# First mixer of a diffusion trunk: probabilities left unscaled, 1/sum applied to the output, two score pairs ahead

## The chip, the cores and the metric

One core of a Trainium2 chip runs the whole program. The metric is the device time of one execution in microseconds; the time before is the median of three runs. One further execution was profiled, and all rows below come from it.

## The reference, cut to what matters

A trunk of two layers works on 256 latent tokens of width 1024 with 256 context tokens beside them. Each layer is half a feed-forward block, a token mixer, and another half feed-forward block. The change lies in the mixer of the first layer only, which joins attention (8 query heads, 2 key and value heads of 64) with four groups of pooling channels:

```
q = rms_norm(q) ; k = rms_norm(k)            # per head of 64
q, k(latent) = rotated by row and column angles
sc = q . k * ATTN_SCALE                      # 256 queries, 512 keys (context + latent)
pr = softmax(sc) ; attn = pr @ v
pool: mean over 2, 4, 8, 16 neighbours minus the token itself, @ pool_w
x = x + gate * (concat(attn, pool) @ w_out)
```

Everything is fp32. Large products are done as three products of a high and a low part of each operand.

## The kernel before, in words

Activations lie transposed, channels on the 128 partitions and tokens on the free axis. A weight block of 128x2048 is loaded by SP's queue into one of two `raw` buffers (`load_w`, L125) and split in two halves: ScalarE casts the high part (L153), VectorE subtracts for the low part (L154). Three buffers each hold high and low parts. A product of 128 outputs over 1024 channels is 24 matmuls of 258 columns (`in_tiles`, `mm3`, L148 to L150). The 8 PSUM banks come from one pool (`bank`, L45).

The mixer (`mixer_a`, L298) projects keys and values first, then four blocks of 128 query channels (`q_proj`); a block t holds query head t (group 0, first 64 partitions) and head t + 4 (group 1, last 64). `k_norm` (L354) sums the squares of each head by a product with a block matrix, which leaves the sum on all 64 partitions, takes the root on ScalarE and the reciprocal on VectorE over 128x512 elements, and scales the keys. `q_rope` (L386) forms the queries' sums (L390) and rotates a block: two multiplications, one product with a permutation (L343), one addition, and a split. The keys' latent half is rotated in `k_rope`. `q_norm` gives the queries' factors, which enter later as the scale of the exponential.

The attention goes by rounds v = 0 to 7: block t = v // 2, query half b = v % 2. `score(v)` makes two score tiles of 128 queries x 512 keys, one per group, in a PSUM bank each (six products, L441); VectorE takes the row maximum (L445) and scales it (L446); ScalarE takes the exponential with the row sum as a second output (L448); VectorE takes the reciprocal of the sum (L450) and multiplies the 512 probabilities with it (L451). `turn(v)` transposes the eight 128x128 pieces on TensorE (L463), and ScalarE copies them to SBUF (L464). After both halves of a block, `attend(t)` multiplies with the values (L472), 64 outputs for each group, and splits the result from PSUM (L153, L154).

The loop issues `score(v + 1)` before `turn(v)`. Between these stand pieces of the pooling branch, listed in `fill`: `p_mm` (24 matmuls, L148 to L150), `p_proj` (VectorE and ScalarE) and `p_finish` (one product, L425). The weight blocks of the output projection are loaded and split in rounds 3, 5 and 6; their VectorE halves are pinned to the program's order. The fourth is loaded in `out_proj`, which follows with 8 x 24 matmuls.

The framework orders the instructions of each engine when the kernel is built: program order is the priority, and a planner with cost estimates lets an instruction go ahead when an earlier one isn't ready by its reckoning. Each engine then runs its list in order. Semaphores and buffer waits are set by the framework.

Of the kernel before, what the change touches and what calls it, by code (L numbers as in the profile page):

```python
# [9 lines left out]
F32 = mybir.dt.float32  # L10
F32R = mybir.dt.float32r
BF16 = mybir.dt.bfloat16
AF = mybir.ActivationFunctionType
ALU = mybir.AluOpType
AX = mybir.AxisListType

P = 128
D = 1024
NK = D // P
T = 256  # L20
# [11 lines left out]
K_BLK, K_ROT, K_COS, K_SIN, K_HSEL, K_END = 0, 128, 256, 512, 768, 770  # L32
# [3 lines left out]
def trunk(ctx: ExitStack, tc: tile.TileContext, I, out):  # L36
    nc = tc.nc
    V, S, PE = nc.vector, nc.scalar, nc.tensor
# [3 lines left out]
    tmp = ctx.enter_context(tc.tile_pool(name="tmp", bufs=1))  # L42
    pp = ctx.enter_context(tc.tile_pool(name="pp", bufs=8, space=bass.MemoryType.PSUM))

    def bank():  # L45
        return pp.tile([P, 512], F32, name="ps")
# [4 lines left out]
    ident = const.tile([P, P], F32, name="ident")  # L51
# [9 lines left out]
    epsb = const.tile([P, 1], F32, name="epsb")  # L61
# [90 lines left out]
    def split(hi, lo, src, pin=lambda ins: ins):  # L152
        S.copy(hi, src)  # L153
        pin(V.tensor_tensor(out=lo, in0=src, in1=hi.bitcast(F32), op=ALU.subtract))  # L154
# [143 lines left out]
    def mixer_a(after):  # L298
        with tc.tile_pool(name="mixa", bufs=1) as mp:
            poolw = mp.tile([P, 4, P], F32, name="poolw")  # L300
            cst = mp.tile([P, K_END], F32, name="cst")
            nc.sync.dma_start(out=cst, in_=I["cst"])
            blk = cst[:, K_BLK:K_BLK + P]
            rot = cst[:, K_ROT:K_ROT + P]
            cosT = cst[:, K_COS:K_COS + T]
            sinT = cst[:, K_SIN:K_SIN + T]
# [27 lines left out]
                                op=ALU.mult)  # L334
                return c

            def rotate(z):

                zs = tmp.tile([P, T], F32, name="hn", bufs=2)
                V.tensor_tensor(out=zs, in0=z, in1=sinT, op=ALU.mult)  # L340
                V.tensor_tensor(out=z, in0=z, in1=cosT, op=ALU.mult)
                ps = bank()
                PE.matmul(ps[:, :T], rot, zs, start=True, stop=True)  # L343
                V.tensor_tensor(out=z, in0=ps[:, :T], in1=z, op=ALU.add)
                return z

            def kv(mh, part, ps):
                z = (kz, vz)[mh][:, part]
# [3 lines left out]
                    S.activation(out=ksq[:, part], in_=z, func=AF.Square)  # L352

            def k_norm():  # L354
                ps = bank()
                PE.matmul(ps, blk, ksq, start=True, stop=True)
                S.activation(out=ksq, in_=ps.rearrange("p (a t) -> p a t", a=2), func=AF.Sqrt, scale=1.0 / 64, bias=epsb)
                V.reciprocal(ksq, ksq)
                V.scalar_tensor_tensor(out=kz, in0=kz, scalar=par[:, C_QK + 1:C_QK + 2],
                                       in1=ksq, op0=ALU.mult, op1=ALU.mult)  # L360

            def k_rope():
                rotate(kz[:, 0])
                split(KH, KL, kz)

            def v_turn():
                ps = bank()
                for i in range(4):
                    PE.transpose(ps[:, i * P:i * P + P],
                                 vz[:, i // 2, i % 2 * P:i % 2 * P + P], ident)  # L370
                S.copy(VV, ps.rearrange("p (i c) -> p i c", i=4))

            qz = {}

            def q_proj(t):
                z = mp.tile([P, T], F32, name="qz", bufs=4)
                sq = mp.tile([P, T], F32, name="qsq", bufs=4)
                c = proj(1 + t // 2, t % 2, z)
                S.activation(out=sq, in_=z, func=AF.Square, bias=c)
                g = par[:, C_QK:C_QK + 1]  # L380
                cg = mp.tile([P, 1], F32, name="col", bufs=8)
                V.tensor_tensor(out=cg, in0=c, in1=g, op=ALU.mult)
                S.activation(out=z, in_=z, func=AF.Identity, scale=g, bias=cg)
                qz[t] = (z, sq)

            def q_rope(t):  # L386
                z, sq = qz.pop(t)
                for b in range(2):
                    c = 4 * t + 2 * b
                    PE.matmul(qps[:, c:c + 2], sq[:, b * P:b * P + P], hsel, start=True, stop=True)  # L390
                split(QH[:, t], QL[:, t], rotate(z))

            def q_norm():
                q16 = qs.rearrange("p t b h -> p (t b h)")
                S.activation(out=q16, in_=qps[:, 0:16], func=AF.Sqrt, scale=1.0 / 64, bias=epsb)
                V.reciprocal(q16, q16)
                V.tensor_scalar(q16, q16, ATTN_SCALE, None, ALU.mult)
# [3 lines left out]
            def p_proj(gi):  # L401
                w = WINDOWS[gi]
                icnt = mp.tile([P, T], F32, name="icnt", bufs=2)
                nc.sync.dma_start(out=icnt, in_=I["icnt"][gi].partition_broadcast(P))
                pb = mp.tile([P, T + 16], F32, name="pb", bufs=2)
                nc.gpsimd.memset(pb[:, 0:8], 0.0)
                nc.gpsimd.memset(pb[:, 8 + T:], 0.0)
                mid = pb[:, 8:8 + T]
                c = proj(0, 0, mid, pps.pop(gi))
                S.activation(out=mid, in_=mid, func=AF.Identity, bias=c)  # L410
                cur, width, step = pb, T + 16, 1
                while step < w:
                    nxt = mp.tile([P, T + 16], F32, name="pw", bufs=2)
                    V.tensor_tensor(out=nxt[:, :width - step], in0=cur[:, :width - step],
                                    in1=cur[:, step:width], op=ALU.add)
                    cur, width, step = nxt, width - step, 2 * step
                st = 8 - w // 2
                pd = mp.tile([P, T], F32, name="pd", bufs=2)
                V.tensor_tensor(out=pd, in0=cur[:, st:st + T], in1=icnt, op=ALU.mult)
                V.tensor_tensor(out=pd, in0=pd, in1=mid, op=ALU.subtract)  # L420
                pds[gi] = pd
# [9 lines left out]

            pes, pts = {}, {}

            def score(v):
                t, b = v // 2, v % 2
                bs = slice(b * P, b * P + P)
                ps = [bank(), bank()]
                own = [slice(64 * g, 64 * g + 64) for g in range(2)]
                for i, (q, k) in enumerate(((QL, KH), (QH, KH), (QH, KL))):
                    for g in range(2):  # L440
                        PE.matmul(ps[g], q[own[g], t, bs], k[own[g]], start=i == 0, stop=i == 2)  # L441
                for g in range(2):
                    st = mp.tile([P, 3], F32, name="st", bufs=4)
                    sc = qs[:, t, b, g:g + 1]
                    V.reduce_max(out=st[:, 0:1], in_=ps[g], axis=AX.X)  # L445
                    V.tensor_scalar(st[:, 0:1], st[:, 0:1], sc, -1.0, ALU.mult, ALU.mult)  # L446
                    pe = tmp.tile([P, 2 * T], F32, name=("sa", "h32")[g], bufs=2)
                    S.activation(out=pe, in_=ps[g], func=AF.Exp, scale=sc, bias=st[:, 0:1],  # L448
                                 accum_out=st[:, 1:2])
                    V.reciprocal(st[:, 2:3], st[:, 1:2])  # L450
                    V.tensor_scalar(pe, pe, st[:, 2:3], None, ALU.mult)  # L451
                    pes[v, g] = pe

            def turn(v):
                t, b = v // 2, v % 2
# [10 lines left out]
            def attend(t):  # L466
                av = bank()
                pt = [pts.pop((t, g)) for g in range(2)]
                for i in range(4):
                    for g in range(2):  # L470
                        own = slice(64 * g, 64 * g + 64)
                        PE.matmul(av[own, :T], VV[:, i, own], pt[g][:, i], start=i == 0, stop=i == 3)  # L472
                split(OH[:, 4 + t], OL[:, 4 + t], av[:, :T])

            psk = in_tiles(*weights(0), (0, 1), (0, T + 2), T + 2, late=True)
            rstd()
# [6 lines left out]
            def p_mm(gi):  # L483
                pps[gi] = in_tiles(*weights(3 + gi // 2), (gi % 2,), (0,), T + 2)[0]

            k_norm()
            p_mm(0)
            qps = bank()
            q_rope(0)
            q_rope(1)  # L490
            p_mm(1)
            q_rope(2)
            v_turn()
            q_rope(3)
            k_rope()
            q_norm()
            score(0)
            p_proj(0)
            p_proj(1)
            fill = {0: lambda: p_mm(2), 1: lambda: (p_mm(3), p_finish(0), p_proj(2)),  # L500
                    2: lambda: (p_finish(1), p_proj(3)), 3: lambda: p_finish(2),
                    4: lambda: p_finish(3)}
            wout = []
            for v in range(8):
                if v in fill:
                    fill[v]()
                if v + 1 < 8:
                    score(v + 1)
                if v in (3, 5, 6):
                    wout.append(load_w(I["w_out_a"][len(wout)], 2048, tc.keep_in_program_order))  # L510
                turn(v)
                if v % 2 == 0 and v:
                    attend(v // 2 - 1)
# [290 lines left out]
```

## Time and profile before

| | |
|---|---|
| median of 3 runs | 1154.62 us (1152.18 to 1155.01) |
| profiled execution | 1152.68 us, span 1150.9 us |
| TensorE busy | 98% of the span |
| VectorE busy | 874.2 us, 76% |
| ScalarE busy | 521.6 us, 45% |
| mean granted TensorE clock | 0.999 |

The span runs from the first to the last instruction. Busy time counts an engine's instructions; ends of matmuls are modelled, so a matmul's pace is better read from start to start. The waits give idle time of an engine before an instruction and what released it. The first mixer's own work runs from about 407 us to about 503 us, its attention rounds from about 435 us to 480 us.

### The profile page before, as it was taken

The numbers are of one execution on the slowest core, as the hardware profiler recorded it, in microseconds if no ns is written. First come the engines' busy times: TensorE is split into PE (matmuls) and PEld (weight loads), VectorE is DVE, ScalarE is ACT, GpSimd is POOL, SyncE is SP. The second block draws the span as 40 slices with busy tenths as digits, with TensorE's granted clock in tenths as the row PEclk, the third lists the DMA queues.
The fourth block names the chain that finished last, engine by engine and source line by source line (L and its number), as shares of the span: only waits on it lengthen the run. The fifth ranks groups of instructions, "written<-read, shape, count | busy, mean of one in ns | idle before, by whom it ended". The sixth has DMA issues, their size and how long they took to land.

```text
span 1150.9 us, 19103 instructions
## 1 busy us (share of the span) xinstructions
PE 1132.6 (98%) x7646; PEld 1031.1 (90%) x7646; DVE 874.2 (76%) x1614; ACT 521.6 (45%) x814; POOL 68.4 (6%) x140
## 2 busy tenths in 40 slices
PE   8999999999999997899999999999999999999998
PEld 4878888888888895699999999999999899999998
DVE  5967787878789989778778788656767688756663
ACT  5552212222223456565334456434445866534442
POOL 0000110122222100000010000000000000000000
PEclk9999999999999999999999999999999999999999
DMA  8844656788888840556587656446546536546543
GB/s 318 309 147 156 194 185 232 275 299 317 303 289 303 318 159 10 183 183 219 180 312 261 229 193 219 162 155 225 184 142 247 185 132 210 182 152 226 179 146 116
DMA packets 52408, 242.72 MB, mean 211 GB/s; under 512 B 5600, under 2 KB 11488, under 8 KB 38880
## 3 DMA queue, kind: packets, MB, share of 16 engines
q1 hardware_dynamic: 33888, 174.39, 42.8%
q0 software_dynamic: 18432, 67.12, 17.5%
q8 instruction: 60, 0.98, 0.3%
q14 instruction: 28, 0.23, 0.1%
HBM read 240.44 MB, written 1.05 MB: 210 GB/s over the span
## 4 chain that ended last, share of the span: by engine, by line
PE 93%; DVE 4%; ACT 1%; DMA 1%; issue 1%; SPq 0%; ACTq 0%; DVEq 0%
PE ps L148 29%; PE ps L149 29%; PE ps L150 29%; PE ps L662 1%; PE ps L583 1%; PE ps L584 1%; PE ps L582 1%; PE ps L645 1%; DMA raw<-in_w 1%; PE ps L630 1%; DVE st L445 1%; DVE wlo L154 1%; DVE wm L80 1%; DVE junk L80 0%; PE ps L472 0%
## 5 line engine op out<-in xcount | busy, mean ns | idle before, releaser
L148 PE MATMUL ps<-AH,wlo 128*128 128x258 f32 (+2 forms) x1664 | 507.9, 306 | 0.3 <-ACT AH L153 0.3
L149 PE MATMUL ps<-AH,whi 128*128 128x258 f32 (+2 forms) x1664 | 507.2, 305 | 0.0
L150 PE MATMUL ps<-AL,whi 128*128 128x258 f32 (+2 forms) x1664 | 506.1, 305 | 0.0
L153 ACT CAST whi<-raw 128x1024 fp32r<-128x1024 f32 (+2 forms) x354 | 313.6, 921 | 364.5 <-PE ps L150 254.6
L154 DVE TENSOR_TENSOR wlo<-raw,whi 128x1024 fp32r<-128x1024 f32 (+2 forms) x354 | 367.7, 1065 | 53.6 <-ACT whi L153 52.8
L148 PEld LDWEIGHTS ps<-AH,wlo 128*128 128x128 f32 x1664 | 317.1, 191 | 16.3 <-issue 1.0
L149 PEld LDWEIGHTS ps<-AH,whi 128*128 128x128 f32 x1664 | 315.0, 189 | 14.7 <-issue 0.5
L150 PEld LDWEIGHTS ps<-AL,whi 128*128 128x128 f32 x1664 | 314.1, 189 | 14.2 <-DVE AL L154 0.2
L150 PE MATMUL ps<-HL,whi 128*128 128x256 f32 (+1 forms) x704 | 218.0, 310 | 0.0
L149 PE MATMUL ps<-HH,whi 128*128 128x256 f32 (+1 forms) x704 | 218.0, 310 | 0.0
L148 PE MATMUL ps<-HH,wlo 128*128 128x256 f32 (+1 forms) x704 | 218.0, 310 | 0.0
L80 DVE CUSTOM_DVE_ANT_0 wm<-wm,cc 128x1024 f32<-128x1024 f32 x138 | 165.0, 1221 | 6.1 <-DMA wm<-in_w_mod 5.4
L150 PEld LDWEIGHTS ps<-HL,whi 128*128 128x128 f32 x704 | 132.5, 188 | 7.8
L149 PEld LDWEIGHTS ps<-HH,whi 128*128 128x128 f32 x704 | 132.6, 188 | 7.7
L148 PEld LDWEIGHTS ps<-HH,wlo 128*128 128x128 f32 x704 | 132.5, 188 | 7.7
L72 POOL DMA_DIRECT2D wm<-in_w_mod x128 | 67.7, 529 | 553.8 <-DVE mod L80 507.0
L206 ACT ACTIVATE sa<-sa,cb 128x256 f32<-128x256 f32 x66 | 33.6, 510 | 120.4 <-DVE sa L205 117.0
L246 DVE SCALAR_TENSOR_TENSOR X<-ps,gate,X 128x256 f32<-128x256 f32 x64 | 30.9, 483 | 47.4 <-PE ps L150 47.2
L204 DVE COPY cb<-ps 128x1 f32<-128x1 f32 x66 | 10.3, 156 | 73.6 <-PE ps L150 73.5
L80 DVE CUSTOM_DVE_ANT_0 junk<-wm,cc 128x1024 bf16<-128x1024 f32 x34 | 41.5, 1219 | 8.8 <-ACT cc L632 8.1
L212 DVE TENSOR_TENSOR h<-ps,sa 128x512 f32<-128x512 f32 x22 | 15.2, 693 | 42.1 <-PE ps L150 33.6
L154 DVE TENSOR_TENSOR HL<-h,HH 128x256 fp32r<-128x256 f32 (+1 forms) x88 | 42.4, 485 | 0.0
(160 smaller groups left out, 709.5 us busy)
## 6 DMA issues: line engine op xcount, KB each, us to landing
raw<-in_w SPq DMA_DIRECT2D x84, 1024.0 KB, 4.9
wm<-in_w_mod POOLq DMA_DIRECT2D x128, 512.0 KB, 5.0
raw<-in_w SPq DMA_DIRECT2D x64, 704.0 KB, 4.1
wm<-in_w_mod SPq DMA_DIRECT2D x10, 512.0 KB, 6.9
raw<-in_w_in_a SPq DMA_DIRECT2D x5, 1024.0 KB, 8.5
raw<-in_w SPq DMA_DIRECT2D x8, 512.0 KB, 6.2
raw<-in_w_out_a SPq DMA_DIRECT2D x4, 1024.0 KB, 4.8
raw<-in_w_in_cu SPq DMA_DIRECT2D x4, 1024.0 KB, 4.9
```

What stands on the lines that cost most here:

```text
L72: eng.dma_start(out=w, in_=I["w_mod"][layer, i])
L80: pin(V.tensor_tensor_reduce(out=res, in0=w, in1=cc[:, st, :], scale=1.0, scalar=0.0, op0=ALU.mult, op1=ALU.add, accum_out=mod[:, 2 * laye ...
L148: PE.matmul(ps, wl, xh, start=first, stop=False)
L149: PE.matmul(ps, wh, xh, start=False, stop=False)
L150: PE.matmul(ps, wh, xl, start=False, stop=last)
L153: S.copy(hi, src)
L154: pin(V.tensor_tensor(out=lo, in0=src, in1=hi.bitcast(F32), op=ALU.subtract))
L206: S.activation(out=sa[:, :T], in_=sa[:, :T], func=AF.Silu, bias=cb[:, 0:1])
L212: V.tensor_tensor(out=h32[:, :n], in0=ps[1][:, :n], in1=sa[:, :n], op=ALU.mult)
L246: V.scalar_tensor_tensor(out=X[:, m, :T], in0=ps[:, :T], scalar=gate[:, 2 * layer, sub, m:m + 1], in1=X[:, m, :T], op0=ALU.mult, op1=ALU.add)
L445: V.reduce_max(out=st[:, 0:1], in_=ps[g], axis=AX.X)
L582: PE.matmul(ps[b], AL[:, k, ts], hi[:, ws], start=(k == 0), stop=False)
```

## The change

Probabilities stay unscaled: the row sums go to a tile `su` that lasts for the whole mixer, one reciprocal per block gives `ri`, and after the product with the values 1/sum is spread over partitions and applied to the output. The spread is a product: the column of 1/sum, broadcast to 64 columns, is the stationary operand and the identity the moving one, so that each of 64 output partitions gets the 128 values as a row. Four such products serve one block (two query halves, two groups). The keys' 1/rms is now computed on 128x8 elements (tokens on partitions) and spread in the same way by eight products. Rotations take two query blocks at a time. Scores are issued two rounds ahead of the transposes, the queries' sums come first, `p_mm(1)` and `p_mm(2)` stand elsewhere, and the output projection's weights are loaded in rounds 4 and 6, two blocks instead of three.

```diff
             def k_norm():
                 ps = bank()
-                PE.matmul(ps, blk, ksq, start=True, stop=True)
-                S.activation(out=ksq, in_=ps.rearrange("p (a t) -> p a t", a=2), func=AF.Sqrt, scale=1.0 / 64, bias=epsb)
-                V.reciprocal(ksq, ksq)
+                for i in range(4):
+                    PE.matmul(ps[:, 2 * i:2 * i + 2], ksq[:, i // 2, i % 2 * P:i % 2 * P + P], hsel,
+                              start=True, stop=True)
+                rk = mp.tile([P, 8], F32, name="rk")
+                S.activation(out=rk, in_=ps[:, 0:8], func=AF.Sqrt, scale=1.0 / 64, bias=epsb)
+                V.reciprocal(rk, rk)
+                return rk
+
+            def k_scale(rk):
+                ps = spread([rk[:, 2 * i:2 * i + 2] for i in range(4)])
                 V.scalar_tensor_tensor(out=kz, in0=kz, scalar=par[:, C_QK + 1:C_QK + 2],
-                                       in1=ksq, op0=ALU.mult, op1=ALU.mult)
+                                       in1=ps.rearrange("p (a t) -> p a t", a=2),
+                                       op0=ALU.mult, op1=ALU.mult)
+
+            def spread(cols):
+                ps = bank()
+                for i, c in enumerate(cols):
+                    for g in range(2):
+                        PE.matmul(ps[64 * g:64 * g + 64, i * P:i * P + P],
+                                  c[:, g:g + 1].broadcast_to([P, 64]), ident, start=True, stop=True)
+                return ps
...
+            def q_rope(h):
+                z = qz.pop(h)
+                rotate(z, 2)
+                split(QH[:, 2 * h:2 * h + 2], QL[:, 2 * h:2 * h + 2], z)
...
-                    pe = tmp.tile([P, 2 * T], F32, name=("sa", "h32")[g], bufs=2)
+                    pe = tmp.tile([P, 2 * T], F32, name="sa", bufs=2) if v % 3 == 2 else \
+                        mp.tile([P, 2 * T], F32, name="pe", bufs=4)
                     S.activation(out=pe, in_=ps[g], func=AF.Exp, scale=sc, bias=st[:, 0:1],
-                                 accum_out=st[:, 1:2])
-                    V.reciprocal(st[:, 2:3], st[:, 1:2])
-                    V.tensor_scalar(pe, pe, st[:, 2:3], None, ALU.mult)
+                                 accum_out=su[:, t, b, g:g + 1])
                     pes[v, g] = pe
+                if b == 1:
+                    V.reciprocal(ri[:, t], su[:, t])
...
-                split(OH[:, 4 + t], OL[:, 4 + t], av[:, :T])
+                ps = spread([ri[:, t, b] for b in range(2)])
+                rs = tmp.tile([P, T], F32, name="hn", bufs=2)
+                S.copy(rs, ps[:, :T])
+                V.tensor_tensor(out=rs, in0=av[:, :T], in1=rs, op=ALU.mult)
+                split(OH[:, 4 + t], OL[:, 4 + t], rs)
...
-            k_norm()
+            rk = k_norm()
             p_mm(0)
             qps = bank()
+            for t in range(4):
+                q_sums(t)
+            k_scale(rk)
             q_rope(0)
+            q_norm()
+            p_mm(1)
+            k_rope()
+            v_turn()
             q_rope(1)
-            p_mm(1)
-            q_rope(2)
-            v_turn()
-            q_rope(3)
-            k_rope()
-            q_norm()
             score(0)
+            p_mm(2)
+            score(1)
             p_proj(0)
             p_proj(1)
-            fill = {0: lambda: p_mm(2), 1: lambda: (p_mm(3), p_finish(0), p_proj(2)),
-                    2: lambda: (p_finish(1), p_proj(3)), 3: lambda: p_finish(2),
-                    4: lambda: p_finish(3)}
+            fill = {0: lambda: (p_mm(3), p_finish(0)), 1: lambda: (p_finish(1), p_proj(2)),
+                    2: lambda: p_proj(3), 3: lambda: p_finish(2), 5: lambda: p_finish(3)}
             wout = []
             for v in range(8):
+                if v + 2 < 8:
+                    score(v + 2)
                 if v in fill:
                     fill[v]()
-                if v + 1 < 8:
-                    score(v + 1)
-                if v in (3, 5, 6):
+                if v in (4, 6):
                     wout.append(load_w(I["w_out_a"][len(wout)], 2048, tc.keep_in_program_order))
                 turn(v)
```

`rotate` takes n blocks and reads its angle tables broadcast over them; `q_sums(t)` is the sums' part of the old `q_rope`.

## Rows read from the trace of the kernel before

**Rows 1.** The page's first part: busy us, share of the span, instructions.

```profile
PE 1132.6 (98%) x7646; PEld 1031.1 (90%) x7646; DVE 874.2 (76%) x1614; ACT 521.6 (45%) x814; POOL 68.4 (6%) x140
```

**Rows 2.** Stretches: from:to, length, busy by engine (instructions), granted clock, DMA share, GB/s.

```profile
421.40:441.68 20.28, 17.99 (x116) 15.21 (x115) 17.10 (x44) 13.39 (x25) 0.14 (x2) 0.92 0.18 59
441.68:479.28 37.60, 28.49 (x200) 18.46 (x200) 33.75 (x89) 25.19 (x55) 2.24 (x6) 1.00 0.33 118
```

**Rows 3.** TensorE's waits, 400 to 520: us in total, times, longest.

```profile
PE ps L463 <- DVE sa L451: 6.5, 5, 1.9
...
PE ps L463 <- DVE h L451: 1.5, 3, 1.1
```

**Rows 4.** Timeline of TensorE, 432 to 441: start, us, instruction [idle before <-releaser].

```profile
432.71 0.70 PE L343 MATMUL ps<-hn,cst 128*128 128x256 f32 x2 [0.71 <-DVE hn L340]
434.96 1.26 PE L441 MATMUL ps<-wm 64*128 64x512 f32 x6 [1.56 <-ACT wm L153]
436.16 0.58 PE L148 MATMUL ps<-AH,wlo 128*128 128x258 f32 x1
...
439.54 0.29 PE L148 MATMUL ps<-AH,wlo 128*128 128x258 f32 x1
...
440.51 0.29 PE L150 MATMUL ps<-AL,whi 128*128 128x258 f32 x1
```

**Rows 5.** Stretches of 1 us around the first scores, columns as in rows 2.

```profile
437.00:438.00 1.00, 1.00 (x6) 1.00 (x6) 1.00 (x5) 0.98 (x2) 0.00 (x0) 0.50 0.00 0
```

**Rows 6.** VectorE's groups, 421.4 to 482.05: instruction xcount | busy us, mean ns | idle before.

```profile
L154 DVE TENSOR_TENSOR wlo<-raw,whi 128x1024 fp32r<-128x1024 f32 x7 | 8.3, 1220 | 0.0
L451 DVE TENSOR_SCALAR h<-h,st 128x512 f32<-128x512 f32 x8 | 3.9, 484 | 0.1
L451 DVE TENSOR_SCALAR sa<-sa,st 128x512 f32<-128x512 f32 x8 | 3.9, 483 | 0.1
L358 DVE RECIPROCAL X<-X 128x512 f32<-128x512 f32 x1 | 3.4, 3353 | 0.9 <-ACT X L357 0.9
...
L450 DVE RECIPROCAL st<-st 128x1 f32<-128x1 f32 x16 | 2.6, 161 | 1.8 <-ACT sa L448 0.9 <-ACT h L448 0.3
...
L333 DVE TENSOR_TENSOR pb<-ps,rb 128x256 f32<-128x256 f32 x4 | 1.7, 416 | 0.0
```

**Rows 7.** ScalarE's groups, 421.4 to 482.05, columns as in rows 6.

```profile
L464 ACT COPY pt<-ps 128x512 f32<-128x512 f32 x16 | 9.0, 588 | 3.0 <-PE ps L463 3.0
...
L153 ACT CAST AH<-ps 128x256 fp32r<-128x256 f32 x4 | 1.5, 372 | 3.6 <-PE ps L472 3.6
```

**Rows 8.** Line L555 of the second mixer: ns min/median/max, first and last start.

```profile
L555 PE MATMUL ps<-wsp,VT x32: 273/275/377, 929.2 to 932.8; 128*128 128x128 f32 x32
```

**Rows 9.** Timeline of TensorE at 430 and 454, columns as in rows 4.

```profile
429.64 0.95 PE L390 MATMUL ps<-cst,qsq 128*128 128x2 f32 x8
430.45 0.68 PE L343 MATMUL ps<-hn,cst 128*128 128x256 f32 x2
430.97 0.60 PE L369 MATMUL ps<-ident,X 128*128 128x128 f32 x4
...
453.24 0.63 PE L463 MATMUL ps<-ident,h 128*128 128x128 f32 x4 [0.23 <-DVE h L451]
453.80 1.95 PE L472 MATMUL ps<-pt,VV 128*64 128x256 f32 x16
455.68 0.70 PE L425 MATMUL ps<-pd,poolw 128*128 128x256 f32 x2
```

**Rows 10.** Chain that ended last, 421 to 425: start, us, what.

```profile
421.40 0.86 PE ps L356 x2
```

**Rows 11.** Timelines of VectorE and ScalarE for one score pair, columns as in rows 4.

```profile
449.02 1.28 DVE L445 TENSOR_REDUCE st<-ps 128x1 f32<-128x512 f32 x2
...
451.94 0.20 ACT L448 ACTIVATION_READ_ACCUMULATOR h<-ps,st,qs 128x1 f32 x1
```

**Rows 12.** The page's DMA issues: queue, count, KB each, median us to landing.

```profile
raw<-in_w_out_a SPq DMA_DIRECT2D x4, 1024.0 KB, 4.8
```

More of the change, by code (lines that the diff above doesn't have):

```diff
@@ L302, in mixer_a @@
             nc.sync.dma_start(out=cst, in_=I["cst"])
-            blk = cst[:, K_BLK:K_BLK + P]
             rot = cst[:, K_ROT:K_ROT + P]
@@ L335, in proj, with rotate @@
                 return c
[L337 to L345, printed above, removed]
+            def rotate(z, n):
+                zs = tmp.tile([P, 2 * T], F32, name="h32", bufs=2)[:, :n * T]
+                zs3 = zs.rearrange("p (a t) -> p a t", a=n)
+                V.tensor_tensor(out=zs3, in0=z, in1=sinT.unsqueeze(1).broadcast_to([P, n, T]),
+                                op=ALU.mult)
+                V.tensor_tensor(out=z, in0=z, in1=cosT.unsqueeze(1).broadcast_to([P, n, T]),
+                                op=ALU.mult)
+                ps = bank()[:, :n * T]
+                PE.matmul(ps, rot, zs, start=True, stop=True)
+                V.tensor_tensor(out=z, in0=ps.rearrange("p (a t) -> p a t", a=n), in1=z, op=ALU.add)
             def kv(mh, part, ps):
@@ L355, in k_norm @@
                 ps = bank()
-                PE.matmul(ps, blk, ksq, start=True, stop=True)
-                S.activation(out=ksq, in_=ps.rearrange("p (a t) -> p a t", a=2), func=AF.Sqrt, scale=1.0 / 64, bias=epsb)
-                V.reciprocal(ksq, ksq)
-                V.scalar_tensor_tensor(out=kz, in0=kz, scalar=par[:, C_QK + 1:C_QK + 2],
-                                       in1=ksq, op0=ALU.mult, op1=ALU.mult)
+                for i in range(4):
[7 more added lines that the diff above has]
+                ps = spread([rk[:, 2 * i:2 * i + 2] for i in range(4)])
+                V.scalar_tensor_tensor(out=kz, in0=kz, scalar=par[:, C_QK + 1:C_QK + 2],
+                                       in1=ps.rearrange("p (a t) -> p a t", a=2),
[7 more added lines that the diff above has]
+                return ps
             def k_rope():
-                rotate(kz[:, 0])
+                rotate(kz[:, 0:1], 1)
                 split(KH, KL, kz)
@@ L371, in v_turn @@
                 S.copy(VV, ps.rearrange("p (i c) -> p i c", i=4))
-            qz = {}
+            qz, qsq = {}, {}
             def q_proj(t):
-                z = mp.tile([P, T], F32, name="qz", bufs=4)
+                if t % 2 == 0:
+                    qz[t // 2] = mp.tile([P, 2, T], F32, name="qz", bufs=2)
+                z = qz[t // 2][:, t % 2]
                 sq = mp.tile([P, T], F32, name="qsq", bufs=4)
@@ L383, in q_proj, with q_sums @@
                 S.activation(out=z, in_=z, func=AF.Identity, scale=g, bias=cg)
-                qz[t] = (z, sq)
-            def q_rope(t):
-                z, sq = qz.pop(t)
+                qsq[t] = sq
+            def q_sums(t):
+                sq = qsq.pop(t)
                 for b in range(2):
@@ L390, in q_rope @@
                     PE.matmul(qps[:, c:c + 2], sq[:, b * P:b * P + P], hsel, start=True, stop=True)
-                split(QH[:, t], QL[:, t], rotate(z))
+            def q_rope(h):
+                z = qz.pop(h)
+                rotate(z, 2)
+                split(QH[:, 2 * h:2 * h + 2], QL[:, 2 * h:2 * h + 2], z)
             def q_norm():
@@ L432, in mixer_a @@
             pes, pts = {}, {}
+            su = mp.tile([P, 4, 2, 2], F32, name="su")
+            ri = mp.tile([P, 4, 2, 2], F32, name="ri")
             def score(v):
@@ L442, in score @@
                 for g in range(2):
-                    st = mp.tile([P, 3], F32, name="st", bufs=4)
+                    st = mp.tile([P, 1], F32, name="st", bufs=6)
                     sc = qs[:, t, b, g:g + 1]
```

## The prediction

> **What bounds the kernel now.** I read the page's first part, then the busy time of each engine by stretches, then TensorE's waits, then the timelines of the mixer. TensorE is busy for 1132.6 us, 98% of the span [rows 1]: outside the first mixer there is next to nothing to gain. The stretches show where it stands: 20.28 less 17.99 = 2.3 us of idle time from the keys' sums (421.4) to the start of the attention rounds (441.7), and 37.60 less 28.49 = 9.1 us in the rounds, up to the last output product (479.3) [rows 2]. That is 11.4 us. The waits say for whom: 8.0 us are transposes (L463) that wait for VectorE's scaling of the probabilities (L451) [rows 3]. In the rounds VectorE is busy 33.75 of 37.60 us [rows 2]: they are VectorE's, and TensorE takes its pace.
>
> A further loss is no idle time. The timeline shows TensorE waiting 0.71 and 1.56 us around the keys' rotation, with little work between, and then 15 products of 258 columns from 436.16 to 439.54, 0.225 us each, where the next eight, to 440.51, take 0.12 each [rows 4]. The granted clock there is 0.50, the lower of its two levels, 1.2 GHz [rows 5]; in the rounds it is 1.00 [rows 2]. Fifteen products at 0.12 are 1.8 us; 3.4 went by: 1.6 lost.
>
> **The change part by part.**
>
> *Normalising moved onto the output.* Gone are 16 multiplications of 128x512 (L451, 3.9 + 3.9 us) and 16 reciprocals (L450, 2.6). Added on VectorE are 4 reciprocals (at L450's 0.16: 0.6) and 4 multiplications by 1/sum out of PSUM (at L333's 0.42: 1.7) [rows 6]: 8 us less. With one weight block fewer in the rounds (two L154 halves, 2.4) about 23 of 33.75 are left, and VectorE no longer sets the pace. ScalarE gets 4 copies of 128x256 out of PSUM (0.37 as L153's [rows 7]: 1.5) on its 25.19.
>
> *The price on TensorE*: four identity products with 64 outputs and 128 columns per head block and eight for the keys, 24 in all, each fp32 and so two records. No row shows this form. From above: L555 has the same 128 columns, but 128 outputs; its 32 records go from 929.2 to 932.8, 0.116 each, 0.23 a product, 5.6 for 24 [rows 8]. From below: L472 has the same half-array form on 256 columns; its 16 records fill 453.80 to 455.68, 0.117 each, where a full-array fp32 record of 256 columns (L343) takes 0.26 (two from 430.45 to 430.97) [rows 9]: two halves run at once. Half the columns at that pace are 0.06, 0.12 a product, 2.9 in all. I take 0.15 (nearer to L472, whose form it is): 1.2 for the keys and 2.4 for the output, 3.6.
>
> A change of form costs nothing that the trace shows: the L472 group begins 0.56 after four transposes that are 0.63 long by their own record (453.24) [rows 9]. The Trainium skill (TensorEngine Tiling (Array Packing), Key Properties) says that a change of tiling mode drains TensorE, which speaks against 64-output products between full ones. By it the keys' spread would pay two such drains and the output's none, as they follow L472 in its own mode; the trace puts no gap there, and the sum keeps its terms.
>
> *Keys' 1/rms on 8 columns.* Gone: the reciprocal of 128x512 (3.35 us of VectorE, L358 [rows 6]), which stands before the rotations of the queries in its queue, and L356's two records (0.86 us). Added: four products of two columns; eight records of that kind (L390) filled 429.64 to 430.45, 0.81, so the trade on TensorE is nought [rows 9, 10]. The root and the reciprocal shrink to 8 columns. The scaling itself stays and now waits for the spread, behind p_mm(0) and the queries' sums; behind it in VectorE's queue stands the first rotation, and for that waits TensorE's rotation product. The cover: VectorE has lost 3.35 us of work before that point, and TensorE has p_mm(1)'s 2.9 us to go on with. I cost it at nothing; without the cover it would be the keys' scaling and two multiplications, 1.6 us at some 0.7, 0.42 and 0.42.
>
> *Rotation by pairs.* The queries' twelve VectorE instructions of 256 columns become six of 512, and four splits become two: fewer fixed parts, the same elements, all beside TensorE's work. Nothing is counted, up or down by 0.5 us.
>
> *Order.* p_mm(1), 24 products of 0.12, moves to behind the first rotation, so that the keys' rotation runs beside 2.9 us of products; p_mm(2) stands between the first two score pairs. I count the 2.3 us of idle time and the 1.6 of lower clock as gone, less 0.3 for the keys' split, which the first scores still wait for.
>
> *Two score pairs ahead.* From the start of a pair's two reduces (449.02) to the end of its second exponential's sum (451.94 + 0.20) it is 3.1 us [rows 11]. Between a pair's scores and its transposes then stand another pair's scores (about 1), two transposed blocks (1.1 by 453.24), half an output with its spread (1.2) and mostly a fill: 3.3 us or more, and the normalising that followed is gone. So the rounds lose most of their 9.1 us. What stays: the last block's copy before the last output products; the tail (copy, multiply, cast, subtract at 0.37, 0.42, 0.37, 0.42: 1.6 us against 2.5 us of output projection that needs no result of it); and rounds in which two halves of a weight block (2.4) stand before a reduce in VectorE's queue. I leave 1.7 us for all, somewhat under the longest of today's waits (1.9 [rows 3]).
>
> *Weights of the output projection.* Three blocks are split in the rounds now, two then. SP's queue carries these loads and then those of the next stage through two raw buffers, so the third and fourth block and the next stage's first start when a split ends. A load lands 4.8 us after its issue [rows 12], its split takes some 3.6 more (three halves at L154's 1.2, since casts run beside subtractions); the third block is wanted 11.5 us into the projection (96 products of 0.12). That leaves 3 us even if its load began with the projection. Cost nothing; without the cover each us late is one lost.
>
> **Sum** against the profiled execution (1152.68 us, 1.8 of it outside the span): 11.4 + 1.6 - 3.6 - 0.3 - 1.7 = 7.4 us less, 1145.3. The median of the runs is 1.9 above that execution; against it the forecast is 1147.2.
>
> **The rivals.**
>
> *ScalarE takes over the rounds.* It is busy 25.19 of 37.60 us and gains 1.5. Its waits for transposes (L464, 3.0 us) and for output products (L153, 3.6) [rows 7] are a round trip with TensorE that a second pair ahead doesn't shorten. If 6.6 of TensorE's 9.1 us stay on that account, the gain is 2.5 - 2.4 in the rounds and 2.3 + 1.6 - 1.2 - 0.3 in front, 2.5 us: 1152.1. For it: weight casts stand in ScalarE's queue too. Against: today's waits name VectorE.
>
> *Slower: PSUM banks.* The pool has eight. Two score pairs hold four, p_mm(2) and p_mm(3) two until rounds 1 and 2, a transposed pair two, an output with its spread two. In rounds 0, 1, 2, 4 and 6 that is all of them, and the next product waits until a pair's exponentials are through, 3.1 us [rows 11]. Five such waits are 15.5; 15.5 + 3.6 - 11.4 - 1.6 = 6.1 us slower, 1160.7. It decides from 9.4 us of such waits on. Against it: with VectorE's 8 us gone, a pair's exponentials end before the pair two further on is due. The Trainium skill (PSUM — Partial Sum Buffer, Summary: rules for kernel authors) asks to evacuate promptly; here the sums of p_mm(2) and p_mm(3) lie through a round and more.
>
> *It doesn't do what it says.* The order on each engine is a planner's; today it joined the sums of two query blocks (eight L390 records in a row at 429.64 [rows 9]), between which the code has a rotation. It may place p_mm(1) and p_mm(2) so that the low clock stays (1.6) with 2.3 us of idle time: gain 3.5, 1151.1.
>
> *Better than forecast*: products at 2.9 and nothing left over, 11.4 + 1.6 - 2.9 = 10.1: 1144.5. The modelled ends of products before a wait (four transposes that are 0.63 long but step by 0.56) may hide a little more idle time at each: 2 us over the rounds at most, 1142.5.
>
> **How the numbers follow.** Forecast 0.5 (its own range 1144.5 to 1150), better 0.17, ScalarE 0.14, planner 0.09, banks 0.1. What can be told from no change is 0.3%, 3.5 us: under 1151.1 is faster. Forecast and better hold 0.67; half of the planner's case and a fourth of ScalarE's come to it: 0.75. The rest of these two is the same, with a bank case of few waits: 0.16. Slower 0.09. The range goes from the better case, 1142, to just under the median, 1154.
>
> **What would show it.** Right: no L451, no stretch at 0.50 around the first scores, TensorE's waits from 421 to the end of the rounds under 3 us and none for VectorE over 1, score pairs two ahead of their transposes, spread products at 0.12 to 0.23 us. Wrong: waits of score products or of p_mm's first product for exponentials (banks), of transposes for them (ScalarE), or output-projection products that wait for the third weight block.

## The result, and the profile after

The changed kernel takes 1141.76 us (median of 4, 1141.21 to 1142.81) against 1153.55 of the kernel before (median of 4): a ratio of 0.9899, 95% interval 0.9881 to 0.9916. That is some 11.7 us less (11.8 by the medians), where 7.4 was forecast, and 0.24 us below the range. The profiled execution took 1142.17 us, 10.5 less than that of before.

The page's first part and the stretches (columns as in [rows 1, 2]; from the keys' sums to the second scores, then to the end of the last output product):

```profile
PE 1132.2 (99%) x7696; PEld 1033.9 (91%) x7696; DVE 863.6 (76%) x1582; ACT 522.0 (46%) x816; POOL 68.4 (6%) x140
```

```profile
420.37:437.49 17.12, 16.71 (x130) 14.23 (x128) 13.13 (x34) 11.98 (x21) 0.14 (x2) 1.00 0.20 70
437.49:468.41 30.92, 30.04 (x236) 22.41 (x235) 26.98 (x67) 26.09 (x60) 2.23 (x6) 1.00 0.31 117
```

VectorE's load in the rounds fell from 33.75 us [rows 2] to 26.98; the two cuts do not hold quite the same work, as the new one takes in the second scores. From the keys' sums to the first result of the output projection, the same work but for the change, VectorE is busy for 41.15 us, before for 51.44. TensorE is busy for 30.04 of 30.92. Its waits in the mixer are down from 11.3 us to 1.3 in three pieces, none of them for VectorE (columns as in [rows 3]; L501 is the output product, L469 the scores):

```profile
PE ps L501 <- ACT pt L493: 0.9, 2, 0.5
PE ps L469 <- ACT wm L153: 0.4, 1, 0.4
```

TensorE's timeline (columns as in [rows 4]) has the new products, L377, for the keys and for one output, and products of 258 columns right behind the first scores:

```profile
425.93 1.09 PE L377 MATMUL ps<-ident,rk 128*64 128x128 f32 x16
426.95 1.12 PE L345 MATMUL ps<-h,cst 128*128 128x512 f32 x2
...
433.12 0.73 PE L469 MATMUL ps<-wm 64*128 64x512 f32 x4 [0.41 <-ACT wm L153]
...
434.98 0.28 PE L149 MATMUL ps<-AH,whi 128*128 128x258 f32 x1
435.10 0.29 PE L150 MATMUL ps<-AL,whi 128*128 128x258 f32 x1
...
455.44 1.95 PE L501 MATMUL ps<-pt,VV 128*64 128x256 f32 x16
457.21 0.61 PE L377 MATMUL ps<-ident,ri 128*64 128x128 f32 x8
457.75 0.96 PE L469 MATMUL ps<-wm 64*128 64x512 f32 x6
...
461.02 0.65 PE L501 MATMUL ps<-pt,VV 128*64 128x256 f32 x2
461.50 0.38 PE L377 MATMUL ps<-ident,ri 128*64 128x128 f32 x2
...
464.01 1.09 PE L492 MATMUL ps<-ident,pe 128*128 128x128 f32 x8
```

The keys' 16 records fill 425.93 to 426.95, 0.064 each, and an output's 8 fill 457.21 to 457.75. That output with its spread takes 2.31 us (455.44 to 457.75). The next one comes in pieces and takes 2.99 (461.02 to 464.01), though the view of waits lists nothing there. The 258-column products start every 0.12 us, at a granted clock of 1.00, where those of [rows 4, 5] ran at 0.50:

```profile
435.00:436.00 1.00, 1.00 (x11) 1.00 (x10) 1.00 (x3) 1.00 (x1) 0.00 (x0) 1.00 0.09 16
```

To compare executions I take one stretch in each trace: from the first record of the keys' sums to the first result of the output projection (L292). It is split into TensorE's waits as the view gives them, the time lost at the low clock (length times 1 less the granted clock, by half microseconds), and the rest, which is work and whatever idle time the view doesn't list, as under modelled ends. Before: 421.24 to 482.1. After: 420.37 to 471.6.

| kernel | stretch | waits (count) | lost at 0.50 | rest |
|---|---|---|---|---|
| before, profile at hand | 60.9 | 11.3 (11) | 1.7 | 47.9 |
| before, repeated | 62.4 | 11.3 (11) | 3.4 | 47.7 |
| before, once more | 62.2 | 11.3 (11) | 3.4 | 47.5 |
| after | 51.2 | 1.3 (3) | 0 | 49.9 |
| front_only | 59.6 | 9.1 (10) | 1.7 | 48.8 |
| rounds_only | 53.4 | 3.2 (4) | 1.7 | 48.5 |
| one_ahead | 57.4 | 5.0 (7) | 1.7 | 50.7 |
| scaled | 54.9 | 5.1 (5) | 1.7 | 48.1 |
| spread_twice | 54.2 | 1.6 (3) | 0 | 52.6 |
| seven_banks | 51.0 | 1.1 (3) | 0 | 49.9 |
| attend_late | 50.7 | 1.9 (3) | 0 | 48.8 |
| pmm_moved | 63.3 | 12.3 (12) | 3.4 | 47.6 |
| keys_wide | 52.4 | 2.1 (3) | 1.7 | 48.6 |
| keys_wide_late | 52.1 | 3.5 (5) | 0.3 | 48.3 |

Stretches are read in one execution each; ratios below are timed against the kernel before on the same chip. Executions of the same code before the mixer differ too: the stretch began between 419.86 and 421.63 in these fourteen traces. From its end to the end of the span it is 668.8 to 669.2 us in thirteen of them, so that a span is the start of the stretch, its length and a constant; in `keys_wide_late` it is 670.1, as most of its low stretch lies behind the end of the stretch.

### The profile page after: what moved, and what is told of

It reads as the page before. It is cut to its first block, busy times and chain, and to the rows that moved or that the text cites. A ratio compares the mean times of both kernels' runs of the same rounds, so it can differ in the third digit from the quotient of the medians.

```text
span 1140.4 us, 19165 instructions
## 1 busy us (share of the span) xinstructions
PE 1132.2 (99%) x7696; PEld 1033.9 (91%) x7696; DVE 863.6 (76%) x1582; ACT 522.0 (46%) x816; POOL 68.4 (6%) x140
## 4 chain that ended last, share of the span: by engine, by line
PE 97%; DVE 1%; ACT 1%; DMA 1%; issue 0%; SPq 0%; DVEq 0%; ACTq 0%
PE ps L148 30%; PE ps L149 30%; PE ps L150 30%; PE ps L697 1%; PE ps L618 1%; PE ps L619 1%; PE ps L617 1%; PE ps L680 1%; PE ps L665 1%; DMA raw<-in_w_out_a 0%; ACT whi L153 0%; PE ps L501 0%; PE ps L469 0%; DVE st L473 0%; PE ps L172 0%; ACT pe L477 0%
## 5 line engine op out<-in xcount | busy, mean ns | idle before, releaser
L154 DVE TENSOR_TENSOR wlo<-raw,whi 128x1024 fp32r<-128x1024 f32 (+2 forms) x354 | 367.6, 1064 | 54.4 <-ACT whi L153 53.4
L246 DVE SCALAR_TENSOR_TENSOR X<-ps,gate,X 128x256 f32<-128x256 f32 x64 | 30.9, 482 | 48.0 <-PE ps L150 47.9
```

Of the source, the lines that this page charges most:

```text
L246: V.scalar_tensor_tensor(out=X[:, m, :T], in0=ps[:, :T], scalar=gate[:, 2 * layer, sub, m:m + 1], in1=X[:, m, :T], op0=ALU.mult, op1=ALU.add)
```

## The experiments

**The two halves.** `front_only` is the changed front with the old rounds, `rounds_only` the reverse.

```diff
 front_only, against the changed kernel
-    (score, turn, attend and the loop of the changed kernel)
+    (those of the kernel before)
 rounds_only, against the kernel before
-    (score, turn, attend and the loop of the kernel before)
+    (those of the changed kernel, and spread)
```

> The keys' and queries' front of the changed kernel with the rounds of the kernel before (scaled probabilities, one pair ahead, weight blocks in rounds 3, 5 and 6). Theory (TensorE's idle time and its low clock in front are a gain of their own): first scores 1.0 us sooner after the keys' sums, no stretch at 0.50, the products of p_mm(2) at 0.12 again, 1.6 to 1.9: 2.5 to 3.5 us faster than before. Rival (front and rounds don't add, since VectorE's rounds take what the front gives): under 1 us faster. Rival (the low clock stays, as it comes with the rounds): 1 us faster and a row at 0.50.

> The front of the kernel before with the rounds of the changed one (unscaled probabilities, spread on the output, two pairs ahead, weight blocks in rounds 4 and 6). Theory: the rest of the 9.6 us by which the stretch from the keys' sums to the first output projection result got shorter, 6 to 7.5 us faster than before, with 0.7 and 1.6 us of waits at the keys' rotation and a stretch at 0.50 as before. Rival (parts don't add): either under 5 or over 8.5.

Measured: `front_only` 1150.65 us, 0.9973 (0.9962 to 0.9985), some 3.1 less; `rounds_only` 1145.13, 0.9923 (0.9911 to 0.9936), some 8.9 less. They add to 12.0 against 11.7 for both, so the halves are additive in time, within the intervals. The rounds' 8.9 lies above the 6 to 7.5 expected, while its stretch, 7.4 shorter than that of the profile at hand, lies within; against the two repeats below it is 9.0 and 8.8 shorter. In the traces they don't do what I expected one by one. The front alone shortened its stretch by 1.3 against the profile at hand, not 2.5 to 3.5 (against the repeats by 2.8 and 2.6): its waits fell by 2.2 and the low clock left the first scores, but it came back in the rounds, behind a wait of 1.9, in this execution (columns as in [rows 2]):

```profile
458.00:459.00 1.00, 1.00 (x6) 0.99 (x6) 1.00 (x2) 0.93 (x3) 0.00 (x0) 0.50 0.00 0
459.00:460.00 1.00, 1.00 (x6) 0.65 (x6) 1.00 (x2) 0.73 (x2) 0.00 (x0) 0.50 0.08 16
460.00:461.00 1.00, 1.00 (x6) 0.48 (x4) 1.00 (x4) 0.37 (x1) 0.00 (x0) 0.50 0.00 0
```

The rounds of [rows 2] had a clock of 1.00 with the same products and waits. The low clock is therefore no property of the front.

**The two parts of the rounds.** `one_ahead` takes back the second score pair, `scaled` the unscaled probabilities.

```diff
 one_ahead
-            score(1)
...
-                if v + 2 < 8:
-                    score(v + 2)
                 if v in fill:
                     fill[v]()
+                if v + 1 < 8:
+                    score(v + 1)
 scaled
+                    r1 = ri[:, t, b, g:g + 1]
+                    V.reciprocal(r1, su[:, t, b, g:g + 1])
+                    V.tensor_scalar(pe, pe, r1, None, ALU.mult)
...
-                ps = spread([ri[:, t, b] for b in range(2)])
...
+                split(OH[:, 4 + t], OL[:, 4 + t], av[:, :T])
```

> The changed kernel with scores one round ahead of the transposes. Theory (VectorE's 8 us are most of the rounds' gain, the second pair ahead the smaller part): transposes wait for exponentials in the rounds without a long fill, 2 to 4 us slower than the changed kernel. Rival (the second pair ahead makes the gain): 6 us or more slower. Rival (it does nothing once VectorE is free): within 1 us.

> The changed kernel with the 16 multiplications and reciprocals on the probabilities again and no spread on the output, two pairs ahead. Theory: VectorE has some 35 us of work in rounds that TensorE could do in 29, TensorE saves 2.2 of spread products: 3 to 5 us slower than the changed kernel, waits of transposes for VectorE. Rival (latency, not VectorE's load, was what bound the rounds, so two pairs ahead hide the scaling): 1 to 2 us faster than the changed kernel by the spread saved.

Measured: `one_ahead` 1149.25 us, 0.9954 (0.9941 to 0.9967); `scaled` 1146.52, 0.9936 (0.9922 to 0.9950). TensorE's waits in the mixer, `one_ahead` first (L492 and L493 are the transposes, L477 the exponential, L481 the scaling, L480 the reciprocal):

```profile
PE ps L492 <- ACT pe L477: 3.9, 4, 1.5
PE ps L492 <- ACT sa L477: 0.5, 1, 0.5
PE ps L469 <- ACT wm L153: 0.4, 1, 0.4
PE ps L501 <- ACT pt L493: 0.2, 1, 0.2
```

```profile
PE ps L493 <- DVE pe L481: 2.8, 2, 2.5
PE ps L493 <- DVE ri L480: 1.5, 1, 1.5
PE ps L493 <- DVE st L474: 0.4, 1, 0.4
PE ps L469 <- ACT wm L153: 0.4, 1, 0.4
```

With one pair ahead transposes wait for the exponential itself (4.4 us), with the scaling they wait for VectorE (4.7): two different limits, one of latency and one of load. `scaled` was as expected, 3.7 longer than the changed kernel's stretch. `one_ahead` was not: 6.1 longer, 3.7 of it waits, 1.7 the low clock and 0.7 the rest, so the second pair is worth more than I gave it, and the rival that it makes the gain (6 us or more) fits the size. With `front_only` as neither part, the stretches make a square: neither 59.6, no scaling alone 57.4 (2.2 less, after paying for the spread), two ahead alone 54.9 (4.6 less), both 51.2 (8.3 less, 1.5 more than the two apart). All but the last have one low stretch of 1.7 us, which makes up the 1.5; each is read in one execution, so whether only both parts together keep the clock up is not shown. In listed waits the two parts are alike: 9.1 us become 5.0 without the scaling and 5.1 with two pairs ahead, though VectorE is busy for 41.12 us of the one stretch and 45.99 of the other (47.73 in `front_only`). The scaling's part then pays for the spread, the second pair pays nothing. (`front_only` differs from the others by its fill order and third weight block as well.)

**The price of the spread.** Every spread product is issued twice.

```diff
-                for i, c in enumerate(cols):
+                for i, c in [ic for ic in enumerate(cols) for _ in range(2)]:
```

> The changed kernel with every spread product issued twice into the same place: 24 more. Theory (TensorE is the bound throughout, and its products cost what the trace steps by, 0.13 us each): 3.0 to 3.5 us slower than the changed kernel. Rival (part of them lies under waits for ScalarE): 1.5 us or less. Rival (0.23 each, as the full-array row had it): 5.5.

Measured: 1145.17 us, 0.9929 (0.9916 to 0.9941), by the medians 3.4 above the changed kernel; the stretch is 2.9 longer and the rest 2.6. Its timeline shows 32 records where the changed kernel has 16, in 1.90 us:

```profile
425.89 1.97 PE L377 MATMUL ps<-ident,rk 128*64 128x128 f32 x32
427.79 1.13 PE L345 MATMUL ps<-h,cst 128*128 128x512 f32 x2
```

At 0.064 a record the 48 added records are 3.1 us, so nearly all that is added to TensorE here is added to the time.

**Banks.** One PSUM bank was to be held from before the rounds to their end: an instruction writes to it at the start, and one reads it behind the last output.

```diff
+            held = bank()
+            V.memset(held[:, 0:1], 0.0)
...
             attend(3)
+            keep = mp.tile([P, 1], F32, name="keep")
+            V.tensor_copy(keep, held[:, 0:1])
```

> The changed kernel with one of the eight PSUM banks held through the rounds (two one-column instructions more on VectorE). Theory (banks are no bound: exponentials end well before the pair two further on is due): within 1.5 us of the changed kernel. Rival (the rounds run at the edge of eight banks): 4 us or more slower, with waits of score products or transposes for exponentials and copies.

Measured: 1143.18 us, 0.9906 (0.9893 to 0.9920), not to be told from the changed kernel's 0.9899; the stretch is 51.0 with 1.1 us of waits. But the planner moved the read ahead, so this is no test of seven banks. VectorE's timeline (columns as in [rows 11]) has it at 405.92, 14 us before the keys' sums of that trace (420.07):

```profile
390.83 0.06 DVE L458 MEMSET ps<- 128x1 f32 x1
...
405.92 0.15 DVE L553 COPY keep<-ps 128x1 f32<-128x1 f32 x1
```

That the bank was still held in the rounds is not shown. What speaks against the bank rival is the changed kernel's own trace: none of its three waits is one of scores, transposes or p_mm's products for exponentials. So eight banks do not bind in any listed wait; how close they come to it is open.

**The order alone.** In the kernel before, `p_mm(1)` moves behind the last query rotation.

```diff
-            p_mm(1)
             q_rope(2)
             v_turn()
             q_rope(3)
+            p_mm(1)
             k_rope()
```

> The kernel before with one line moved: p_mm(1) to just before the keys' rotation. Theory (the low clock comes from the sparse stretch of TensorE around the keys' rotation, and products put there keep it away): no row at 0.50, 2 to 4 us faster than before (0.7 + 1.6 of waits partly filled, 1.6 of clock). Rival (the chain of VectorE sets the first scores and the products only move the idle time ahead of them): the clock stays up or not, under 1 us faster.

Measured: 1157.37 us, 1.0027 (1.0015 to 1.0040): slower by 3.1. Both theories missed. The wide reciprocal [rows 6] still stands in VectorE's queue before the last two rotations, and p_mm(1) now comes behind them, so TensorE has no products to go on with: it waits 2.28 us for the third rotation, and the clock falls to 0.50 (timeline as in [rows 4], stretches as in [rows 2]):

```profile
426.38 0.95 PE L390 MATMUL ps<-cst,qsq 128*128 128x2 f32 x8
429.61 1.19 PE L343 MATMUL ps<-hn,cst 128*128 128x256 f32 x2 [2.28 <-DVE hn L340]
```

```profile
430.00:431.00 1.00, 1.00 (x4) 0.71 (x4) 1.00 (x5) 0.00 (x0) 0.00 (x0) 0.50 0.00 0
...
464.00:465.00 1.00, 1.00 (x8) 0.58 (x6) 1.00 (x3) 0.25 (x1) 0.00 (x0) 0.50 0.00 0
```

A second low stretch follows in the rounds, behind the wait of 1.9 us there. This trace is of one of the two faster executions (1154.8, mean clock 0.997); the other four took 1157.2 to 1157.6 at 0.994, below every recorded execution of the kernel before. So more of the 3.1 us goes with the clock than this trace shows. In this place p_mm(1) loses. In `keys_wide` below the reciprocal is as wide, but p_mm(1) follows the first pair's rotation as in the changed kernel, and no rotation waits: the order of the changed kernel doesn't need the narrow keys' sums.

**The kernel before, twice more.** Unchanged.

> The kernel before, unchanged, for another profiled execution. Theory (which of the sparse stretches of TensorE are followed by 3.4 us at 0.50 differs from one execution to the next, and each costs 1.7 us): the time is 1152.2 with one such stretch, as in the profile at hand, or about 1154 with two; the waits are the same 11.3 us. Rival (the low clock comes at the same place in each execution): one stretch at the first scores again, and the spread of the times lies elsewhere.

> The kernel before once more. As for the first repetition: the time and the number of stretches at 0.50 go together, 1.7 us apiece, or (rival) they don't.

Measured: 1153.16 and 1152.68 us. The waits are the same to 0.1 us, but each of the two traces has two low stretches, 3.4 us lost, where the profile at hand has one. From the first of the two, one microsecond of each stretch:

```profile
435.00:436.00 1.00, 1.00 (x5) 0.62 (x4) 0.94 (x3) 0.53 (x2) 0.00 (x0) 0.50 0.04 8
462.00:463.00 1.00, 1.00 (x6) 0.50 (x6) 1.00 (x2) 0.54 (x2) 0.00 (x0) 0.50 0.00 0
```

The times do not follow the count one for one, as these two stretches began a microsecond earlier (420.17 and 419.86 against 421.24); that part of the theory, times of 1152.2 and 1154, did not come out. The mean clock recorded with each timed execution does fit two such stretches: it is 0.997 in 25 and 0.995 in 4 of the 29 executions of the kernel before beside these experiments, and 0.999 in none, which is what the profile at hand had. The four at 0.995 took 1155.4 to 1155.7 us, the others 1152.2 to 1155.4 with a median of 1153.0. The changed kernel has 1.000 in 4 of 4. (The mean takes in the end of the span as well: in `attend_late`'s trace it is 0.999 by a fall at 1139.4, behind TensorE's last product, which costs nothing.)

**Undoing the keys' part, and one output product later.**

```diff
 attend_late
-                if v % 2 == 0 and v:
+                if v % 2 and v > 1:
                     attend(v // 2 - 1)
 keys_wide (with attend_late's line: keys_wide_late)
-            rk = k_norm()
+            k_norm()
...
-            k_scale(rk)
```

(`k_norm` there is that of the kernel before.)

> The changed kernel with each output product one round later (after the transposes of odd rounds), so that it doesn't wait for the copy of the transposes just before it. Theory: the two waits of L501 for ScalarE's copies (0.9 us) shrink or go, 0.5 to 1 us faster than the changed kernel. Rival: the last two outputs meet at the end and the output projection waits for the last one: no gain or up to 1 us slower.

> The changed kernel with the keys' 1/rms on 128x512 elements again (one product with the block matrix, a root and a reciprocal over 512 columns, no spread of eight products). Theory (the keys' spread costs TensorE 1.0 us, and VectorE stood idle 2.2 us before the keys' scaling): the stretch from the keys' sums to the first output projection result 0.5 to 1.0 us shorter than the changed kernel's, the time 0 to 1 us less. Rival (the reciprocal of 3.35 us delays the rotations that TensorE waits for): 1 to 3 us longer, with a wait of the rotation's product for VectorE.

> The same with the output products one round later, the two changes that leave TensorE less to do or to wait for. Theory: they add, 1.0 to 1.6 us less than the changed kernel in that stretch. Rival: no gain, as the waits come back elsewhere.

Measured: `attend_late` 1142.17 us, 0.9898 (0.9885 to 0.9912); `keys_wide` 1143.72, 0.9909 (0.9895 to 0.9923); `keys_wide_late` 1145.25, 0.9925 (0.9912 to 0.9937). The later output product took 0.6 us off the stretch: an output with its spread now takes 2.2 to 2.3 us each time, and the rest is 1.1 less for the same products. But the copies' two waits became one of 1.1 for an exponential and one of 0.4 for the output's low part, and the time is the changed kernel's. `keys_wide` has 1.3 us less of rest, where 1.0 of spread was taken out, and no wait of a rotation's product for VectorE, though the reciprocal is wide again; but the first scores wait longer (first VectorE's reciprocal, then TensorE's waits):

```profile
423.73 3.35 DVE L360 RECIPROCAL X<-X 128x512 f32<-128x512 f32 x1 [1.15 <-ACT X L359]
```

```profile
PE ps L461 <- ACT wm L153: 1.3, 1, 1.3
PE ps L493 <- ACT pt L485: 0.8, 2, 0.4
```

In the traced execution that was followed by a low stretch. Its five times fall in two groups: 1141.6 and 1141.7 with a mean clock of 1.000, and 1143.7, 1143.9 and 1144.2 with 0.998 or 0.999. So neither expectation is met: there is less work for TensorE and a little more waiting, and where the clock falls it takes back more than was saved. `keys_wide_late` has the waits of both and gains nothing, as its rival had it. No version tried beats the changed kernel by what can be measured.

## Why the prediction was wrong

The direction and the place held; the size did not, and the cause held in half. The gain was forecast at 7.4 us and is 11.8; from 1147.2 to 1141.8 are 5.4 us. The step that failed is the sum, as it took one profiled execution for all: its term "1.6 of lower clock" counted the one low stretch of that execution, where both repeats lose 3.4, and its 11.4 us of idle time took the listed waits for all there was. The 1.9 us between that execution and the median was then added as a loss that the change leaves in place.

1. *The low clock.* Both repeats have two low stretches, and their stretch is 62.4 and 62.2 us where the profile at hand has 60.9. The changed kernel has none and 51.2. So the profiled stretch got 9.6 shorter, and against the repeats it is 11.2 and 11.0. The timed gain, 11.8, is 2.2 more than the profiled 9.6. Some 1.5 of this is the second low stretch, if the timed executions had two; their mean clocks fit that, but those executions were not traced. The rest is where the stretch begins, which differs by up to 1.8 us between executions (421.24 and 420.37 in the two profiled ones).

2. *Idle time read from the waits.* 11.4 us were counted as all there was. The rest in the table rose by only 2.1 while 3.2 us of spread were added (the keys' sums are even, 0.81 against 0.86), so 1.1 us net of unlisted idle time went. A part lay under modelled ends: four transposes are 0.66 long by their record, but where the next group need not wait it begins 0.50 behind their start (448.60 and 449.10 in the trace of before). The prediction saw such a part (0.63 long, stepping by 0.56) and put it in the better case instead of in the sum. Shared over the eight waits that went, 1.1 us would be 0.14 each, but how it is really made up was not found. The rest differs by 0.4 among three executions of one kernel, and the new kernel has unlisted idle time of its own: three of its four outputs take 2.8 to 3.0 us, listed waits left out, where the fourth takes 2.31. That is 1.8 us, and it goes when the output comes a round later (`attend_late`).

3. *What stays.* 2.0 us (1.7 + 0.3) were left. Of the listed waits 1.3 stayed: 0.4 before the first scores and 0.5 for the copy before the last output, as said, and 0.4 for a copy within the first output, which was not named. No weight block held up a reduce that TensorE waited for.

4. *The spread.* 3.6 us were put in, 3.2 measured (1.02 for the keys, 0.54 for an output): the lower bound, 2.9, by L472's form [rows 9], was the better guide than the full-array row L555 [rows 8]. No gap stands at the change of form (425.93, the first record right behind the sums), as the prediction read it.

5. *Luck.* Of the 1.9 us, 1.1 was chance: the median of three runs before, 1154.62, became 1153.55 with the fourth.

Points 2 to 4 are 2.2 us, the difference between the 7.4 forecast and the 9.6 of the profiled stretch. With 2.2 from point 1 and 1.1 from point 5 they make up the 5.4 but for rounding.

Of the cause the prediction had half. It read VectorE's 33.75 of 37.60 us as what sets the pace of the rounds. In the square above the second pair ahead takes away as much waiting, 4.0 us, as the scaling does, 4.1, with VectorE nearly as busy as without it. By these traces about half of what TensorE waited out was the time from scores to probabilities, and not how much VectorE had to do. The sum did not suffer, as the change does both. VectorE was not freed as far as reckoned either: 26.98 us in the new cut of the rounds, where about 23 were expected.

Of the rivals, ScalarE's is right in kind: all three listed waits left are for it. It is wrong in that a second pair ahead does shorten its round trip: with one pair ahead the transposes and outputs wait 4.6 us for ScalarE (`one_ahead`), with two 0.9. Banks: no listed wait for one in the changed kernel; that fewer than eight were held is not shown. The planner did shift things (it put the last two products of the first scores behind the first of p_mm(2)), with no wait there.

*Keys' 1/rms* was costed at nothing beside its spread. Undone (`keys_wide`), it saves TensorE's 1.0 us of spread and lengthens a wait by 0.9, and the time is the same within what can be measured: no part of the gain is shown to come from it. *Rotation by pairs* was not tried alone.

## What to carry to other kernels

Where an engine's waits are spread over a dense stretch, take them as a lower bound: add the part hidden under modelled ends, look for groups that take longer than the same group elsewhere, and ask from more than one execution whether the clock fell behind them. Removing a wait can be worth more than its length, and saving work can be worth less than it, if a wait grows beside it. A busy engine beside a waiting one need not be what it waits for: take away its load and the latency one at a time. And where a planner orders the instructions, the trace says whether an experiment held what it was to hold. A profiled execution that is faster than the median may lack a loss that the change removes; then the offset must not be carried over.

## What the runs showed of the hardware

The granted clock fell to 0.50 in stretches that cost 1.7 us each, in the same program after the same waits in some executions and not in others: the wait of 1.9 us at 460 was followed by one in both repeats of the kernel before and not in the profile at hand. Before twelve of the thirteen falls in or just behind the stretches of the table TensorE had stood idle for 1.3 to 2.5 us in one piece (in `pmm_moved` the first fall came within it); in `keys_wide_late` it had three short waits instead (0.2, 0.4 and 0.5 from 471 to 473). The changed kernel, whose longest wait in the mixer is 0.5, had no fall there, and neither had `attend_late` with one of 1.1. What decides it in a given execution was not found.
